# Indexer queries from position 64 on, with both activation parts in one matmul

## The chip, the cores and the metric

The kernel runs on one core of a Trainium2 chip. The metric is the time of one execution on the device in microseconds; the time before is the median of three runs.

## What is computed

One decoder layer over 272 positions (16 meta tokens and 256 of the sequence) of width 2048: sparse attention over a shared latent, a pooling branch, an output projection, a gated feed-forward network and two normalisations. The part that matters here is the indexer, which chooses 64 keys for each query (`top_k = min(256, 256 // 4)`):

```python
dots = jnp.einsum('bqhd,bsd->bqhs', qi, k_idx)
score = jnp.einsum('bqhs,bqh->bqs', jax.nn.relu(dots), wi).astype(jnp.float32)
causal = key_pos[None, :] <= t[:, None]
score = jnp.where(causal[None], score, NEG_INF)
_, sel = lax.top_k(score, top_k)
```

`qi` is the layer's input times 1024 columns of `w_in`, 16 heads of 64. A query at a position below 64 has no more than 64 admissible keys, so all of them are chosen whatever the scores are, and the others are masked again when the logits are made.

## The kernel before, in words

Float32 operands are cut into an upper part, rounded to the chip's `float32r` format (the shapes say fp32r), and a lower part, the rest; a product is the sum of upper by upper, upper by lower and lower by upper. ScalarE makes the upper part of each weight tile (L185) and VectorE the lower one by a subtraction (L186), in two pieces a tile; the tile is called `whl`, its raw form `wraw`. SyncE issues the loads of weight tiles of 1 MB (L191). Three raw and three cut tiles are held at a time, so a tile's cutting can begin when TensorE is done with the tile three before.

The input's cut parts stay in SBUF as 16 K steps (`x_parts`, tile name `xp`, class `Parts`): two stretches of 272 columns, 274 apart. `product` (L288 to L300) runs over K steps and issues three matmuls for each.

The indexer's queries are made in eight tiles of 128 rows, two heads each (the loop over `j` below). A query tile accumulates in PSUM (`mm`) over 16 K steps of three matmuls with 256 columns, for the positions from 16 on. Then ScalarE rounds each head's half to `qi` (L485) and VectorE subtracts it for the lower part (L487); `qi` holds, for a head, the upper part on 64 partitions and the lower on the other 64. While tile j is made, `dots` (L451 to L466) takes the two heads of tile j − 1: head 0 after nine K steps, head 1 after twelve. A head's four matmuls (L460, L461) multiply `qi` with the indexer's keys `kidx`: two for the first 128 queries with 256 key columns, of which 144 are read, and two for the others with 272. ScalarE applies the relu (L463, L464) and VectorE adds to `score` (L466).

During tile 0 and 1 the latent is normalised as well, and in tile 2 TensorE makes a small bias product (L441) from two small loads, `rb_sb` and `oh`, that SyncE issues on the same queue as the weights (L437, L439). The small buffers called "t" (`rl`, `rb_sb`, `oh` and others) are four. After the eight tiles follow the key product (L501 to L503, with the last dot products between), the value product, the choice of keys on VectorE (L554, L555) beside the projection of the attention queries, and all the rest of the layer.

Each engine runs its own instructions in order. That order is made by the tile framework when the program is built, from the order of the code, the edges between tiles, and the free buffers.

Of the kernel before, what the change touches and what calls it, by code (L numbers as in the profile page):

```python
# [11 lines left out]
F32 = mybir.dt.float32  # L12
F32R = mybir.dt.float32r
AF = mybir.ActivationFunctionType
ALU = mybir.AluOpType
AX = mybir.AxisListType

P = 128
D = 2048
NM = 16  # L20
S = 256
T = NM + S
Q0 = NM - 2
NQ = T - Q0
KT = D // P
# [4 lines left out]
DI = 64  # L30
WINS = (2, 4, 8, 16)
TOPK = min(256, S // 4)
FF = 5632
FT = FF // P
PARTS = (8, 8, 8, 8, 8, 4)
# [8 lines left out]
KA = NM + P  # L44
# [23 lines left out]
class Split:  # L68
# [3 lines left out]
    def __init__(self, tile, upper, lower, turned=False, lead=None, early=False, steps=0):  # L72

        self.tile, self.places, self.turned, self.lead, self.early, self.first = tile, (upper, lower), turned, lead, early, P * steps

    def __getitem__(self, key):
        rows, part, c = key
        o = self.places[part]
        if self.lead is not None:
            n = self.first  # L80
            assert c.stop <= n or c.start >= n
            o = self.lead + (n + 64) * part if c.stop <= n else self.places[0] + n + 128 + (2048 - n) * part
        return self.tile[rows, o + c.start:o + (2 * 1024 + 2 if c.stop is None else c.stop)]


class Parts:


    def __init__(self, slot, first, width, apart=274):
        flat = slot.rearrange("p a b -> p (a b)")  # L90
        self.parts = [flat[:, a:a + width] for a in (first, first + apart)]

    def __getitem__(self, key):
        return self.parts[key[1]][key[0], key[2]]
# [35 lines left out]
K_PROJ = (1, 3, 5, 7, 9, 11, 13, 15, 0, 2, 4, 6, 8, 10, 12, 14)  # L130
# [5 lines left out]
def tile_layer(ctx, tc, xt, w_first, w_proj, w_uk, w_uv, w_pool, w_o, w_up, w_down, cols, rows, rel_bias, onehot, out):  # L136
    nc = tc.nc
# [7 lines left out]
    def big():  # L145
        return pm.tile([P, 512], F32, tag="mm", name="mm")

    def small():
        return pa.tile([P, 512], F32, tag="at", name="at")
# [3 lines left out]
    ps = small()  # L153
# [9 lines left out]
    for item in plan:  # L163
# [3 lines left out]
        elif item[0] == "down":  # L167
            n = PARTS[FAST]
# [42 lines left out]
    def split_tile(where=(0, 2048)):  # L211

        return Split(wp.tile([P, 4288], F32R, tag="whl", name="whl"), *where)
# [44 lines left out]
    def weights(ahead=2):  # L258
        i = state["use"]
        state["use"] += 1  # L260
        prefetch(i + 1 + ahead)
        return ready.pop(i)
# [26 lines left out]
    def product(ps, hl, act, lo, hi, places, ks=None, k0=0, k1=KT, firsts=()):  # L289

        for n in range(k0, k1):
            k = (places if ks is None else ks)[n]
            w = slice(P * places.index(k), P * places.index(k) + P)
            wh, wl = hl[:, 0, w], hl[:, 1, w]
            ah, al = act[k][:, 0, lo:hi], act[k][:, 1, lo:hi]
            turned = hl.early if hl.lead is not None and w.start < hl.first else hl.turned
            turn = firsts[n] if n < len(firsts) else "hlx" if turned else "hxl"
            terms = {"h": (wh, ah), "x": (wh, al), "l": (wl, ah)}
            for i, (a, b) in enumerate(terms[t] for t in turn):
                nc.tensor.matmul(ps, a, b, start=n == 0 and i == 0, stop=i == 2 and n == KT - 1)  # L300

    at = ctx.enter_context(ExitStack())
    ap_ = at.enter_context(tc.tile_pool(name="attn", bufs=1))


    x_parts, first = [], []
    for k0, k1 in [(k, k + 1) for k in range(9)] + [(9, 12), (12, 15), (15, 16)]:
# [6 lines left out]
        if k0 % 6 == 0:  # L314
            hl = split_tile()
        for w in ((slice(0, T), slice(T, T + MF)) if k0 == 0 else (slice(0, T + MF),)):
            nc.sync.dma_start(raw[:, k0 % 3:k0 % 3 + k1 - k0, w], w_first[k0:k1, :, w].rearrange("k p c -> p k c"))
        for k in range(k0, k1):
            xk, wk, a0 = raw[:, k % 3, :T], raw[:, k % 3, T:], k % 6 // 3 * 1024 + k % 3 * MF
            c = slice(a0, a0 + MF)  # L320
            a = Parts(ring.tile([P, 2, WIDE], F32R, tag="act", name="xp"), 20, T)
# [35 lines left out]
    def temp(shape, name):  # L357
        return ap_.tile(shape, F32, tag="t", name=name, bufs=4, padded_shape=[P, KW])
# [6 lines left out]
    for k, (hl, a0) in enumerate(first):  # L365
# [4 lines left out]
        for t, (ps, a, m) in terms:  # L370
            nc.tensor.matmul(ps[:m, :T], hl[:, t // 2, a0 + a:a0 + a + m], x_parts[k][:, t % 2, :],  # L371
                             start=k == 0 and t == 0, stop=k == KT - 1 and t == 2)
    ps = heads[0][0]
# [5 lines left out]
    for i in range(2):  # L379
        nc.vector.tensor_tensor(kidx[DI * i:DI * i + DI, 1 + i, :], ps[:DI, :T], kidx[:DI, 0, :].bitcast(F32),  # L380
                                op=ALU.subtract)
# [14 lines left out]
    for j in range(2):  # L396
        ps = heads[1 + j][0]
# [6 lines left out]
    ps = small()  # L404
# [7 lines left out]
    def latent_scale():  # L412
        r = temp([P, W], "r")
        to_partitions(r, sum_rows(sqs))
        nc.vector.tensor_scalar(v, r[:, ::32], 1.0 / C, EPS, op0=ALU.mult, op1=ALU.add)
        nc.gpsimd.tensor_tensor(v, v, half, op=ALU.pow)

    def latent_norm():
        rb = temp([P, W], "rb")
        to_row(rb, v)  # L420
        for j in range(2):
            nc.vector.scalar_tensor_tensor(ct[:, j, :], ct[:, j, :], col(G_KV, j), rb[:, :T], op0=ALU.mult,
                                           op1=ALU.mult)
            nc.scalar.activation(ctp[:, j, 0, :], ct[:, j, :], AF.Copy)
            nc.vector.tensor_tensor(ctp[:, j, 1, :], ct[:, j, :], ctp[:, j, 0, :].bitcast(F32), op=ALU.subtract)
# [28 lines left out]
    def dots(j, qi, pa_, heads, buffer=small):  # L454

        for i in heads:
            h = 2 * j + i
            pb = buffer()
            for o, n, t in ((pa_[:, S * i:S * i + S], S, slice(0, P)), (pb[:, :T], T, slice(P, S))):
                nc.tensor.matmul(o, qi[:, i, t], kidx[:, 0, :n], start=True, stop=False)  # L460
                nc.tensor.matmul(o, qi[:, i, t], kidx[:, 1 + i, :n], start=False, stop=True)  # L461
            rl = temp([P, KW], "rl")
            nc.scalar.activation(rl[:, :KA], pa_[:, S * i:S * i + KA], AF.Relu)  # L463
            nc.scalar.activation(rl[:, KA:], pb[:, :T], AF.Relu)  # L464
            for i2, (a, b) in enumerate(((0, KA), (KA, KW))):
                nc.vector.scalar_tensor_tensor(score[:, a:b], rl[:, a:b], widx[:, i2, h:h + 1], score[:, a:b],  # L466
                                               op0=ALU.mult, op1=ALU.add)

    queries = sb.tile([P, 2, 2, S], F32R, name="qi", tag="y", padded_shape=[P, 2, 2, KT * T // 4])
    qis = []  # L470
    for j in range(8):
        hl = weights()
        ps = big()
        product(ps[:, :S], hl, x_parts, NM, T, K_PROJ, k1=9)
        if j:
            pa_ = small()
            dots(j - 1, qis[j - 1], pa_, (0,))
        product(ps[:, :S], hl, x_parts, NM, T, K_PROJ, k0=9, k1=12)
        if j:
            dots(j - 1, qis[j - 1], pa_, (1,))  # L480
        product(ps[:, :S], hl, x_parts, NM, T, K_PROJ, k0=12)
        qi = queries[:, j % 2]
        for i in range(2):
            r, o = slice(DI * i, DI * i + DI), slice(DI - DI * i, 2 * DI - DI * i)
            query = nc.scalar.activation(qi[r, i, :], ps[r, :S], AF.Copy)  # L485
            query = getattr(query, "ins", query)
            nc.vector.tensor_tensor(qi[o, i, :], ps[r, :S], qi[r, i, :].bitcast(F32), op=ALU.subtract)  # L487
        qis.append(qi)
        if j == 0:
            latent_scale()  # L490
        if j == 1:
            latent_norm()
            relative_bias()
# [3 lines left out]
    for h in range(H):  # L497
        ps = small()
        for c in range(2):
            w = slice(1024 * c + h * HD, 1024 * c + h * HD + HD)  # L500
# [20 lines left out]
    for i, (a, b) in enumerate(((0, NM), (NM, NM + P), (NM + P, T))):  # L521
# [6 lines left out]
        for g in range(2):  # L528
            ps = small()
            for c in range(2):  # L530
                w = slice(1024 * c + 512 * g, 1024 * c + 512 * g + 512)
# [7 lines left out]
            w = slice(512 * g, 512 * g + 512)  # L539
# [10 lines left out]
    src = score  # L550
    for r in range(TOPK // 8):
        for a, b in ((0, KA), (KA, KW)):
# [10 lines left out]
    for h in range(H):  # L563
        hl = weights()
        ps = big()
# [5 lines left out]
    ps = small()  # L571
# [120 lines left out]
    for h in range(H):  # L692
# [3 lines left out]
        hl = weights()  # L696
        ps = big()
# [74 lines left out]
    for m in range(1, KT):  # L772
# [5 lines left out]
        if m == KC:  # L778
            ps = small()
# [151 lines left out]
    gated, todo, both, pair, downs = [], [], [], None, None  # L931
    for item in plan:
# [3 lines left out]
        if item[0] == "down":  # L936
            _, part, c, g = item
            hl = weights()
# [6 lines left out]
            n = PARTS[part]  # L945
            for k in range(4 * g, 4 * g + 4):
                w = slice(512 * (k - 4 * g), 512 * (k - 4 * g) + 512)
                for i in range(2):
                    a, r = pairs[part][k // 2][f"a{i + 1}{k % 2 + 1}"]
# [10 lines left out]
        if half_ == 0:  # L960
            if f % 2 == 0:
                pair = fp.tile([P, 2, S], F32, name="za", tag="z0", bufs=3)
            both = []
        hl = weights()
        ps = big()

        b = 2 * (f - FOLDED) + half_
# [12 lines left out]
        if todo and f > FOLDED + half_:  # L980
            p, r = todo.pop(0)
            with behind(state["use"]):
                pairs[p].append(forms(r, len(pairs[p]), p == FAST))
        if f < FOLDED:
            k = 0
            if f + half_ == 0:
                product(ps[:, :NE], hl, folded, 0, NE, K_UP, k1=5)
                deviation()
                k = 5
# [7 lines left out]
            both = [conv(i * FT + f, i, unfold(both[i]), pair[:, f % 2]) for i in range(2)]  # L997
# [7 lines left out]
        if part > FAST:  # L1005
            a = fp.tile([P, 2, WIDE], F32R, name="gp", tag="gp", bufs=16)
# [5 lines left out]
    n = PARTS[-1]  # L1012
# [3 lines left out]
    for r in range(2):  # L1016
        for c in range(4):
            t = fp.tile([P, 512], F32, name="gb", tag="gp", bufs=16, padded_shape=[P, 2 * WIDE])
# [82 lines left out]
    for i in range(2):  # L1101
        t, mv = slice(i * P, (i + 1) * P), mvs[i]
        waiting = []
        for q, (a, b) in enumerate(cuts[i]):
            ps = small() if i else big()
# [96 lines left out]
```

## Time and profile before

| | |
|---|---|
| median of 3 runs | 1019.71 us (1019.67 to 1019.96) |
| span of the profiled execution | 1019.7 us |
| TensorE matmul busy | 1011.8 us, 99% |
| TensorE weight loads busy | 964.3 us, 95% |
| VectorE busy | 889.8 us, 87% |
| ScalarE busy | 619.5 us, 61% |
| GpSimd busy | 193.4 us, 19% |

The profile lists each engine's busy time, the chain of work that ended last, groups of equal instructions and a timeline with starts from the span's beginning. For the profiled execution it gives the span alone, the time from the first to the last instruction. Matmuls are pipelined: a matmul's recorded length is longer than the distance to the next one's start, so paces are read from starts. In rows, PE is TensorE, PEld its weight loads, DVE VectorE, ACT ScalarE, POOL GpSimd, SP SyncE, and a q behind a name is that engine's queue.

### The profile page before, as it was taken

To read this page: it belongs to the slowest core of one execution; us is meant where nothing else is said; L and a number is where in the kernel's file an instruction comes from. 1 tells how busy PE (TensorE), PEld (TensorE's weight loads), DVE (VectorE), ACT (ScalarE), POOL (GpSimd) and SP (SyncE) were. 2 spreads that over 40 slices of the span, in tenths; PEclk is the share of its full clock that TensorE was granted. 3 is DMA by queue.
4 is the path that set the end of the run, shared out by engine and by line. 5 is a ranking of instruction groups with operands and counts; after the bars stand their busy time and mean duration, and the time that the engine had idled before them with its cause. 6 is when DMAs were issued, how large, how long until landed. Compare 5 with 4: busy or idle time off the path is not lost.

```text
span 1019.7 us, 19201 instructions
## 1 busy us (share of the span) xinstructions
PE 1011.8 (99%) x7644; PEld 964.3 (95%) x7644; DVE 889.8 (87%) x1401; ACT 619.5 (61%) x1000; POOL 193.4 (19%) x245
## 2 busy tenths in 40 slices
PE   9999999999999999999999999999999999999997
PEld 9999999999999999999999999999999999999986
DVE  6878668758869998999999999999999999999876
ACT  7666446645548756655665656656556565666665
POOL 1200014125430021112121111211112111220031
PEclk9999999999999999999999999999999999999999
DMA  9755643354553569899888798887988879888565
GB/s 332 255 190 205 245 148 113 137 187 166 207 206 125 205 197 274 267 370 312 275 281 279 278 304 276 287 276 277 300 281 282 279 279 299 280 285 277 202 218 160
DMA packets 59754, 250.28 MB, mean 245 GB/s; under 512 B 21734, under 2 KB 22416, under 8 KB 32656
## 3 DMA queue, kind: packets, MB, share of 16 engines
q1 hardware_dynamic: 34592, 230.42, 62.2%
q0 software_dynamic: 7888, 16.14, 8.3%
q10 hardware_dynamic: 17184, 2.49, 1.5%
q8 instruction: 60, 0.98, 0.4%
q14 instruction: 30, 0.25, 0.1%
HBM read 232.50 MB, written 2.11 MB: 230 GB/s over the span
## 4 chain that ended last, share of the span: by engine, by line
PE 94%; issue 2%; DVE 1%; DMA 1%; POOL 1%; ACT 0%; POOLq 0%; SPq 0%; DVEq 0%; ACTq 0%
PE mm L300 71%; PE at L899 6%; PE at L898 6%; PE at L900 6%; PE mm L371 2%; DMA wraw<-in_w_down 1%; DVE whl L186 1%; POOL gb L1021 0%; PE mm L599 0%; PE at L460 0%; PE at L634 0%; PE at L461 0%; PE at L346 0%; DVE whl_r L235 0%; DMA wraw<-in_w_first 0%
## 5 line engine op out<-in xcount | busy, mean ns | idle before, releaser
L300 PEld LDWEIGHTS mm<-hp,whl 128*128 128x128 f32 x3840 | 456.9, 188 | 6.3
L300 PE MATMUL mm<-hp,whl 128*128 128x258 f32 x3840 | 458.9, 279 | 0.0
L186 DVE TENSOR_TENSOR whl<-wraw,whl 128x1024 fp32r<-128x1024 f32 (+2 forms) x312 | 370.9, 1216 | 36.9 <-ACT whl L185 35.8
L185 ACT ACTIVATE whl<-wraw 128x1024 fp32r<-128x1024 f32 (+2 forms) x312 | 304.1, 1021 | 76.3 <-PE mm L300 24.6
L300 PE MATMUL mm<-xp,whl 128*128 128x256 f32 (+5 forms) x1152 | 147.1, 284 | 0.0
L300 PEld LDWEIGHTS mm<-xp,whl 128*128 128x128 f32 x1152 | 140.2, 188 | 1.5 <-issue 0.5
L186 DVE TENSOR_TENSOR whl<-room,whl 128x512 fp32r<-128x512 f32 (+1 forms) x104 | 117.8, 1162 | 1.9 <-ACT whl L185 1.6
L185 ACT ACTIVATE whl<-room 128x512 fp32r<-128x512 f32 (+1 forms) x104 | 98.4, 993 | 14.8 <-DVE room L197 7.5
L829 ACT ACTIVATE z<-mm,cv 128x256 f32<-128x256 f32 x40 | 22.6, 565 | 89.7 <-PE mm L300 89.7
L871 POOL TENSOR_TENSOR forms<-za 128x128 f32<-128x128 f32 x20 | 20.4, 1018 | 293.1 <-DVE za L847 228.3
L829 ACT ACTIVATE za<-mm,cv 128x256 f32<-128x256 f32 x40 | 22.6, 565 | 85.1 <-PE mm L300 83.7
L899 PE MATMUL at<-whl,gp 128*128 128x512 f32 x180 | 70.6, 393 | 0.0
L900 PE MATMUL at<-whl,gp 128*128 128x512 f32 x180 | 70.4, 392 | 0.0
L898 PE MATMUL at<-whl,gp 128*128 128x512 f32 x180 | 68.7, 392 | 0.0
L874 POOL TENSOR_TENSOR forms<-za 128x128 f32<-128x128 f32 x20 | 24.4, 1222 | 196.9 <-DVE za L847 144.3
L300 PE MATMUL mm<-mixp,whl 128*128 128x258 f32 x384 | 48.5, 281 | 0.0
L300 PE MATMUL mm<-mixa,whl 128*128 128x258 f32 x384 | 47.8, 280 | 0.0
L300 PEld LDWEIGHTS mm<-mixp,whl 128*128 128x128 f32 x384 | 46.5, 188 | 0.1
L300 PEld LDWEIGHTS mm<-mixa,whl 128*128 128x128 f32 x384 | 46.3, 188 | 0.0
L300 PE MATMUL mm<-fold,whl 128*128 128x260 f32 x384 | 45.8, 280 | 0.0
L300 PEld LDWEIGHTS mm<-fold,whl 128*128 128x128 f32 x384 | 45.5, 187 | 0.1
L900 PEld LDWEIGHTS at<-whl,gp 128*128 128x128 f32 x180 | 33.9, 188 | 7.2
(335 smaller groups left out, 1343.8 us busy)
## 6 DMA issues: line engine op xcount, KB each, us to landing
wraw<-in_w_up SPq DMA_DIRECT2D x62, 1024.0 KB, 5.3
wraw<-in_w_down SPq DMA_DIRECT2D x54, 1024.0 KB, 6.3
room<-in_w_up SPq DMA_DIRECT2D x26, 1024.0 KB, 5.1
room<-in_w_down SPq DMA_DIRECT2D x26, 1024.0 KB, 6.5
wraw<-in_w_proj SPq DMA_DIRECT2D x24, 1024.0 KB, 5.0
wraw<-in_w_o SPq DMA_DIRECT2D x16, 1024.0 KB, 4.8
y<-v POOLq DMA_DIRECT2D x27, 256.0 KB, 8.3
y<-u POOLq DMA_DIRECT2D x18, 256.0 KB, 5.0
```

Source lines behind the costliest of these rows:

```text
L185: upper = nc.scalar.activation(hl[:, 0, c], raw[:, c], AF.Copy)
L186: lower = nc.vector.tensor_tensor(hl[:, 1, c], raw[:, c], hl[:, 0, c].bitcast(F32), op=ALU.subtract)
L300: nc.tensor.matmul(ps, a, b, start=n == 0 and i == 0, stop=i == 2 and n == KT - 1)
L371: nc.tensor.matmul(ps[:m, :T], hl[:, t // 2, a0 + a:a0 + a + m], x_parts[k][:, t % 2, :], start=k == 0 and t == 0, stop=k == KT - 1 and t ...
L829: nc.scalar.activation(z, src[:, 2:NQ], AF.Identity, bias=col(C_B, j), scale=col(C_W, 3 * j + 2))
L871: nc.gpsimd.tensor_tensor(s[:, 0], a21, a22, op=ALU.add)
L874: nc.gpsimd.tensor_tensor(s[:, 3], a11, a21, op=ALU.subtract)
L898: nc.tensor.matmul(ps, a[:, 0, i], hl[:, 0, w], start=j == 0, stop=False)
L899: nc.tensor.matmul(ps, a[:, 0, i], hl[:, 1, w], start=False, stop=False)
L900: nc.tensor.matmul(ps, a[:, 1, i], hl[:, 0, w], start=False, stop=j == n - 1)
```

## The change

Queries are made for the 208 positions from 64 on (`NI = 272 − 64`); the first 48 columns of `qi` are cleared once. For each K step one matmul multiplies the upper weight part with both activation parts side by side, 2 × 208 columns, and a second one adds the lower weight part times the upper activation part, 208 columns, to the second half of the same PSUM range. After the 16 steps ScalarE copies the second half to SBUF (`whole`), VectorE adds the first, and rounding and subtraction read `whole` where they read PSUM. The dot products of the first 128 queries use 144 key columns in place of 256.

```diff
+ALL = TOPK - NM
+NI = S - ALL
...
+        self.whole = (flat, first, apart)
+
+    def both(self, lo, hi):
+
+        flat, first, apart = self.whole
+        return flat[:, first:first + 2 * apart].rearrange("p (a b) -> p a b", b=apart)[:, :, lo:hi]
...
+    def paired(ps, hl, act, lo, hi, places, k0=0, k1=KT):
+
+        m = hi - lo
+        for n in range(k0, k1):
+            k = places[n]
+            w = slice(P * n, P * n + P)
+            nc.tensor.matmul(ps[:, :2 * m], hl[:, 0, w], act[k].both(lo, hi), start=n == 0, stop=False)
+            nc.tensor.matmul(ps[:, m:2 * m], hl[:, 1, w], act[k][:, 0, lo:hi], start=False, stop=n == KT - 1)
+
...
-            for o, n, t in ((pa_[:, S * i:S * i + S], S, slice(0, P)), (pb[:, :T], T, slice(P, S))):
+            for o, n, t in ((pa_[:, S * i:S * i + KA], KA, slice(0, P)), (pb[:, :T], T, slice(P, S))):
...
+    nc.gpsimd.memset(queries[:, :, :, :ALL].bitcast(F32), 0.0)
...
-        product(ps[:, :S], hl, x_parts, NM, T, K_PROJ, k1=9)
+        paired(ps, hl, x_parts, TOPK, T, K_PROJ, k1=9)
...
-        product(ps[:, :S], hl, x_parts, NM, T, K_PROJ, k0=9, k1=12)
+        paired(ps, hl, x_parts, TOPK, T, K_PROJ, k0=9, k1=12)
...
-        product(ps[:, :S], hl, x_parts, NM, T, K_PROJ, k0=12)
+        paired(ps, hl, x_parts, TOPK, T, K_PROJ, k0=12)
         qi = queries[:, j % 2]
+        whole = temp([P, NI], "whole")
+        nc.scalar.activation(whole, ps[:, NI:2 * NI], AF.Copy)
+        nc.vector.tensor_tensor(whole, ps[:, :NI], whole, op=ALU.add)
         for i in range(2):
             r, o = slice(DI * i, DI * i + DI), slice(DI - DI * i, 2 * DI - DI * i)
-            query = nc.scalar.activation(qi[r, i, :], ps[r, :S], AF.Copy)
+            query = nc.scalar.activation(qi[r, i, ALL:], whole[r], AF.Copy)
             query = getattr(query, "ins", query)
-            nc.vector.tensor_tensor(qi[o, i, :], ps[r, :S], qi[r, i, :].bitcast(F32), op=ALU.subtract)
+            nc.vector.tensor_tensor(qi[o, i, ALL:], whole[r], qi[r, i, ALL:].bitcast(F32), op=ALU.subtract)
```

The change also moves instructions, because the framework orders them anew. (Line numbers after the change are higher: L186 is now L194, L191 is L199, L466 is L483, L487 is L508.) On VectorE, at the end of a middle tile, there stood before the change:

```order
L466 SCALAR_TENSOR_TENSOR score<-rl,widx,score 128x272
L487 TENSOR_TENSOR qi<-mm,qi 64x256
L186 TENSOR_TENSOR whl<-wraw,whl 128x1024
L487 TENSOR_TENSOR qi<-mm,qi 64x256
L186 TENSOR_TENSOR whl<-wraw,whl 128x1024
L466 SCALAR_TENSOR_TENSOR score<-rl,widx,score 128x144
```

and now there stands:

```order
L483 SCALAR_TENSOR_TENSOR score<-rl,widx,score 128x272
L503 TENSOR_TENSOR whole<-mm,whole 128x208
L194 TENSOR_TENSOR whl<-wraw,whl 128x1024
L508 TENSOR_TENSOR qi<-whole,qi 64x208 x2
L194 TENSOR_TENSOR whl<-wraw,whl 128x1024
L483 SCALAR_TENSOR_TENSOR score<-rl,widx,score 128x144
```

The subtraction for head 0 was ahead of the first half of the weight split and is now behind it; the add of the two ranges has its old place. On ScalarE it is alike: copy, first half of the split, then both roundings. After tile 6, on VectorE, the split has pieces of 512 and 1536 columns, and the rows now are:

```order
L503 TENSOR_TENSOR whole<-mm,whole 128x208
L194 TENSOR_TENSOR whl<-wraw,whl 128x512
L194 TENSOR_TENSOR whl<-wraw,whl 128x1536
L508 TENSOR_TENSOR qi<-whole,qi 64x208 x2
L483 SCALAR_TENSOR_TENSOR score<-rl,widx,score 128x144
```

Both pieces are now ahead of the subtractions; before, head 0's stood ahead of both and head 1's behind both. On SyncE, where the stage's loads are issued, there stood before:

```order
L331 DMA cv<-in_cols 128x394
L191 DMA wraw<-in_w_proj 128x2048 x6
L437 DMA rb_sb<-in_rel_bias 32x8
L439 DMA oh<-in_onehot 32x272
L191 DMA wraw<-in_w_proj 128x2048 x2
```

and now:

```order
L348 DMA cv<-in_cols 128x394
L199 DMA wraw<-in_w_proj 128x2048 x7
L454 DMA rb_sb<-in_rel_bias 32x8
L456 DMA oh<-in_onehot 32x272
L199 DMA wraw<-in_w_proj 128x2048
```

The two small loads are now issued after the seventh weight tile in place of the sixth.

## Rows read from the trace of the kernel before

**Rows 1.** The page, part 4: the chain that ended last, shares by engine.
```profile
PE 94%; issue 2%; DVE 1%; DMA 1%; POOL 1%; ACT 0%; POOLq 0%; SPq 0%; DVEq 0%; ACTq 0%
```

**Rows 2.** Busy time by stretch: length, engines (instructions), granted clock, DMA share, GB/s.
```profile
23.00:30.00 7.00, 7.00 (x56) 6.63 (x56) 6.91 (x10) 6.22 (x12) 0.00 (x0) 1.00 0.77 253
...
70.20:77.20 7.00, 6.88 (x59) 6.71 (x58) 4.88 (x8) 3.83 (x8) 0.00 (x0) 1.00 0.52 186
```

**Rows 3.** Timeline, TensorE, tiles 2 and 3: start us, length us, engine, line.
```profile
42.51 4.71 PE L300 MATMUL mm<-xp,whl 128*128 128x256 f32 x39
...
47.06 0.28 PE L460 MATMUL at<-kidx,qi 128*128 128x256 f32 x1
...
47.54 1.21 PE L300 MATMUL mm<-xp,whl 128*128 128x256 f32 x9
...
49.08 2.05 PE L300 MATMUL mm<-xp,whl 128*128 128x256 f32 x16
```

**Rows 4.** Timeline, TensorE, feed-forward part: four matmuls of 512 columns, then another.
```profile
404.60 0.39 PE L899 MATMUL at<-whl,gp 128*128 128x512 f32 x1
...
405.51 0.28 PE L300 MATMUL mm<-hp,whl 128*128 128x258 f32 x1
```

**Rows 5.** Weight loads by shape: count | busy us, mean ns of one | idle before.
```profile
L300 PEld LDWEIGHTS mm<-xp,whl 128*128 128x128 f32 x1152 | 140.2, 188 | 1.5 <-issue 0.5
...
L573 PEld LDWEIGHTS at<-kt,qt 128*2 128x2 f32 x16 | 0.5, 82 | 0.3
```

**Rows 6.** Timeline, ScalarE and VectorE at the end of tile 2.
```profile
44.13 0.38 ACT L485 ACTIVATE qi<-mm 64x256 fp32r<-64x256 f32 x1 [1.03 <-PE mm L300]
...
44.42 1.05 ACT L185 ACTIVATE whl<-wraw 128x1024 fp32r<-128x1024 f32 x1
44.55 0.42 DVE L487 TENSOR_TENSOR qi<-mm,qi 64x256 fp32r<-64x256 f32 x1 [0.31 <-ACT qi L485]
...
45.50 1.23 DVE L186 TENSOR_TENSOR whl<-wraw,whl 128x1024 fp32r<-128x1024 f32 x1 [0.53 <-ACT whl L185]
```

**Rows 7.** Timeline, VectorE in tiles 0 and 1, and TensorE's first dot products.
```profile
26.80 3.49 DVE L186 TENSOR_TENSOR whl<-wraw,whl 128x1024 fp32r<-128x1024 f32 x3
...
30.76 0.48 DVE L351 STREAM_TRANSPOSE r<-at 128x288 f32<-128x288 f32 x1
...
33.13 0.28 PE L460 MATMUL at<-kidx,qi 128*128 128x256 f32 x1
```

**Rows 8.** DMA issues from 18 to 48 us (us to landing); timeline of tile 2, TensorE.
```profile
wraw<-in_w_proj SPq DMA_DIRECT2D x6, 1024.0 KB, 5.1
...
oh<-in_onehot SPq DMA_DIRECT2D x1, 34.0 KB, 1.9
...
38.06 0.62 PE L441 MATMUL at<-oh,rb_sb 32*8 32x272 f32 x2
...
40.49 0.28 PE L460 MATMUL at<-kidx,qi 128*128 128x256 f32 x1
```

**Rows 9.** Timeline of tile 7: ScalarE, VectorE, TensorE.
```profile
70.77 2.00 ACT L185 ACTIVATE whl<-wraw 128x512 fp32r<-128x512 f32 x2
...
72.80 1.76 DVE L186 TENSOR_TENSOR whl<-wraw,whl 128x1536 fp32r<-128x1536 f32 x1 [0.69 <-ACT whl L185]
...
74.59 0.43 DVE L487 TENSOR_TENSOR qi<-mm,qi 64x256 fp32r<-64x256 f32 x1
...
75.16 0.35 PE L460 MATMUL at<-kidx,qi 128*128 128x256 f32 x1
...
77.18 0.28 PE L501 MATMUL at<-ctp,whl 128*128 128x272 f32 x1
```

**Rows 10.** Timeline, TensorE: a plain float32 product, two records of one matmul.
```profile
147.27 0.41 PE L598 MATMUL mm<-kt,qt 128*128 128x144 f32 x2
147.51 0.62 PE L599 MATMUL mm<-kt,qt 128*128 128x272 f32 x2
```

**Rows 11.** Timeline, TensorE between the key product's heads.
```profile
80.86 0.39 PE L460 MATMUL mm<-kidx,qi 128*128 128x256 f32 x1
```

## The prediction

> **What bounds the kernel now.** I read the page first: 94% of the chain that ended last is TensorE's work [rows 1]. That says where time can be saved, not that a saving arrives. So the second view is the table of stretches: in the stage of the eight query tiles TensorE has hardly any idle time at the full granted clock, 2.4 GHz, but VectorE is nearly full too in the first stretch (6.91 of 7 us) and 70% full in the last one, 4.88 of 7 [rows 2]. The third view is the timeline of one tile, for the two numbers on which all rests: how fast TensorE streams, and how long before it needs a result that result is there.
>
> Streaming: 39 matmuls of 256 columns start within 47.06 − 42.51 us, 116.7 ns each [rows 3]; 512 columns take (405.51 − 404.60)/4 = 227.5 ns [rows 4]. A line through both gives 0.433 ns a column: 186 ns for 416 columns, and 96 for 208 if the line goes on below 256, which no row shows.
>
> Let E be the moment when a tile's last product has streamed and the next tile may begin. For tile 2, E = 42.51 + 12 × 0.1167 = 43.91 us; for tile 3, 49.08 + 12 × 0.1167 = 50.48: a period of 6.57 us [rows 3]. TensorE comes to head 0's dot products at 47.06 = E + 3.15. What they need is done at 44.55 + 0.42 = E + 1.06 [rows 6]: 2.1 us of slack, because the first subtraction stands ahead of the weight split on VectorE.
>
> **The change, part by part.**
>
> *K steps.* Three matmuls of 256 columns (350 ns) become one of 416 and one of 208. The narrow one lasts 96 ns by the line, but each matmul has a weight load of its own, and those loads last 188 ns for 128 columns and 82 for 2 [rows 5]: 0.84 ns a column above a fixed part, 108 ns for 128 columns. A load that has only a 208-column matmul to hide behind would set the pace. I take 108, because a 256-column matmul's 117 hides exactly such a load now; the bounds are 96 and 117. A K step is then 294 ns, 56 less than before. Over 8 × 16 steps TensorE has 7.2 us less to do (8.7 at 96 ns, 6.0 at 117). The Trainium skill ("TensorE: Matmul & The Clock Gate", LDWEIGHTS) has a load last its columns divided by 1.2 GHz, 107 ns for 128, and so speaks against this change where the line of rows alone does not; by the rule the sum below is 1020.3, by the line 1019.0.
>
> *Dot products.* 32 matmuls of 256 columns become 144: about 10 ns less each at the load's pace, 0.3 us; on the line 32 × (117 − 68) = 1.6.
>
> *The end of a tile.* Now ScalarE copies the second range (0.35 us, a little under the 0.38 of 256 columns), VectorE adds (0.37, as the old subtraction's 0.42 of 256 columns), ScalarE rounds, VectorE subtracts (0.37 each) [rows 6]. And VectorE's queue has the half weight split *between* the add and both subtractions, as the order shows. From E: ScalarE's copy ends at 0.22 + 0.35 = 0.57; the add runs from 0.60 to 0.97; ScalarE's half split starts 0.25 after the copy's start, lasts 1.05 and ends at 1.53; VectorE's half runs from 1.56 to 2.79; the subtraction to 3.19; TensorE starts 0.14 after that (75.16 against 74.59 + 0.43) [rows 9]: E + 3.33. Its nine K steps take 9 × 0.294 = 2.65. So it waits 0.7 us in each tile, and the period is 3.33 + 2 × 0.46 for the heads' dot products (0.48 now [rows 3]) + 7 × 0.294 = 6.31: **0.26 less than before, not 0.9**. VectorE's queue is the bound.
>
> *Tiles 0 and 1.* Tile 0 saves 16 × 56 ns = 0.9 us. But VectorE splits weights until 30.29 in any case [rows 7]; then add 0.37, transposition 0.48, half split 1.23, subtraction 0.37 and gaps end at 32.85, and the dot products start at 33.0 against 33.13: only 0.1 is left. Seven K steps to the tile's end bring 0.4. Balance −0.5.
>
> *Tile 2.* Here TensorE has the small bias product (L441), which needs two small transfers. On SyncE's queue they now stand behind the seventh weight tile instead of the sixth, as the order shows. That tile is issued when VectorE has finished the next half split: 32.85, second subtraction 0.40 with its gap, about 0.17 of small work, 1.23, so 34.7; 5.1 us to landing gives 39.8, and the small ones land behind it [rows 8]. TensorE would be there at about 37.6 (33.0 + 2 × 0.46 + 7 K steps, then five and a wide matmul) and sits until 39.9, where it passed at 38.06 before; then 0.55 for the product, a narrow matmul and three K steps to the dot products: 41.5 against 40.49, **+1.0**. (If they did not queue behind the tile, the second would land 1.9 us after an issue near 35.5, and the term would be −0.4; VectorE's subtractions near 39 hide under this wait and would then be next.) Seven K steps and the dot products bring 0.5 back: balance +0.5.
>
> *Tiles 3 to 6.* 4 × −0.26: balance −0.5.
>
> *Tile 7.* The split queued here has a piece of 512 and one of 1536, and now both stand ahead of the subtractions: ScalarE's two last 2.00 us and end at E + 2.47, VectorE's large one 1.76 more, the subtraction ends at 4.65, the dot products start at E + 4.8. Before, head 0 passed freely and only head 1 waited, and the tile lasted from 70.20 (50.48 and three periods) to 77.18, 6.98 us [rows 9]; now 4.8 + 0.92 + 2.06 = 7.78, **+0.8**: balance +0.3.
>
> *After the tiles.* ScalarE rounds the last tile only after VectorE's add, so its copies of the keys begin about 0.3 later. TensorE already waits in this place (the matmul at 80.86 is 0.39 long where its like are 0.28) [rows 11] and would wait that much more: balance +0.6. Behind it TensorE has the order of before, so the shift stays to the end. POOL's new clearing of 48 columns hides in its idle time (0.00 busy until 30 us [rows 2]); without that cover it would delay tile 0's first rounding, where VectorE is busy until 30.29 anyway.
>
> Sum: the balance runs −0.5, +0.5, −0.5, +0.3 and ends at **+0.6 us**. Against the profiled execution's 1019.7 (the median of the runs is 1019.71) that is **1020.3 us**. At 96 ns a narrow matmul the period is 3.33 + 2 × 0.39 + 7 × 0.282 = 6.08 and the same walk ends at −0.7 (1019.0); at 117, at +1.3 (1021.0). A measurement of this kernel can tell 0.2%, 2.0 us, from no change. With half a microsecond either way for the waits that I worked out, the forecast's own range is 1018.0 to 1021.7.
>
> **The rivals.**
>
> *The work saved arrives.* If the first subtraction ended before E + 2.6 in every tile and the small transfers came in time, TensorE's 7.2 + 0.3 us would come off but for the 0.3 at the end: 1012.5; at 96 ns, 1009.7. For it: TensorE is the engine without idle time [rows 2]. Against: VectorE's 1.23 us in its queue's order, which needs ScalarE's 1.05 first.
>
> *Narrow matmuls run at another pace (the slower side).* A plain float32 matmul of 144 columns is two records that take 0.24 us together [rows 10], 1.69 ns a column. Were the rounded format to fall to that pace below 256 columns, a narrow matmul would last 352 ns: 128 × (352 + 186 − 350) = +24 us and 32 × (244 − 117) ns = +4 for the dot products, with no wait for VectorE left: about 1048. For it: every rounded matmul of the weights that I found has 256 columns or more. Against: 256 and 512 lie on a line that nearly meets zero, as one pass does. It decides from about 128 ns a narrow matmul on, since each 10 ns above mine cost 0.7 us.
>
> *The waits cost the clock.* TensorE would have two waits of some 2 us where it now has none. If the granted clock fell to 1.2 GHz after one for half a tile, 24 of the old matmuls' work would take 117 ns longer each: +2.8, 1023. Against: the clock is 1.00 in every stretch, the last one with short waits included [rows 2]. That idle gaps between bursts lower it is what the same page of the Trainium skill says ("Why this matters for your kernels"); no row here has such a gap.
>
> *The wide matmul gains nothing.* If its two pieces, 274 columns apart, stream like two matmuls, a K step is 2 × 117 + 108 = 342 ns, and mostly the waits stay: 1022.4.
>
> **How the numbers follow.** Forecast 0.70; work arrives 0.13; slow narrow matmuls 0.06; clock 0.06; wide gains nothing 0.05. The first lies within 0.2%, the second is faster, the others slower: 0.13, 0.70, 0.17. The range takes the forecast's own, half a microsecond more below for waits partly escaped, and above reaches to the wide matmul's and the clock's cases: 1017.5 to 1023.0. Left out are the full saving and the slow pace, 0.19.
>
> **What would show it.** TensorE idle for 0.7 us before the first dot products of each tile, released by VectorE's subtraction; a wait of over 2 us at the bias product, for a transfer; the longest wait for VectorE in tile 7; matmuls of 208 columns spaced 108 ns, weight loads still 188. Wrong if tiles come 5.6 us apart, or if narrow matmuls are spaced over 130 ns.

## The result and the profile after

| | before | after |
|---|---|---|
| median of the runs | 1019.79 us (4) | 1025.88 us (4; 1024.10 to 1026.09) |
| ratio, 95% interval | | 1.0055 [1.0041, 1.0069] |
| span of the profiled execution | 1019.7 us | 1024.3 us (its own time 1026.09) |

The change is slower by 0.55%, outside the range of the prediction. Where the time goes is seen by the start of the same work on TensorE, read from both timelines (a line of dot products is that of head 0):

| TensorE starts | before, us | after, us | shift |
|---|---|---|---|
| query tile 0 | 22.95 | 23.50 | +0.55 |
| dot products in tile 1 | 33.13 | 32.79 | −0.34 |
| in tile 2 | 40.49 | 44.84 | +4.35 |
| in tile 3 | 47.06 | 52.84 | +5.78 |
| in tile 6 | 66.78 | 72.11 | +5.33 |
| in tile 7 | 73.35 | 80.03 | +6.68 |
| key product | 77.18 | 83.18 | +6.00 |
| value product | 84.47 | 91.16 | +6.69 |
| attention queries | 91.87 | 98.57 | +6.70 |
| end of the span | 1019.7 | 1024.3 | +4.6 |

Nearly all is lost in one tile and a half: 6.1 of the 6.7 us lie between the dot products in tile 1 and those in tile 3. The chain that ended last, after (answers to [rows 1]): 4% of it have gone from TensorE to other engines and to transfers. That is where the path now runs, not time lost.

```profile
PE 90%; DVE 3%; DMA 3%; issue 2%; ACT 1%; POOL 1%; SPq 0%; POOLq 0%; ACTq 0%; DVEq 0%
```

Busy time by stretch, after, columns as in [rows 2] (the number before the DMA share is the granted clock):

```profile
23.00:30.00 7.00, 6.72 (x45) 6.22 (x43) 6.83 (x9) 6.49 (x12) 0.00 (x0) 1.00 0.71 224
36.50:44.00 7.50, 3.41 (x15) 2.24 (x14) 5.69 (x11) 3.17 (x6) 2.15 (x3) 0.85 0.42 137
44.00:50.50 6.50, 6.50 (x32) 6.41 (x32) 2.03 (x5) 2.04 (x6) 2.88 (x4) 0.65 0.55 185
...
46.00:47.50 1.50, 1.50 (x7) 1.45 (x7) 0.64 (x2) 0.39 (x1) 0.14 (x1) 0.50 0.13 47
...
50.50:57.00 6.50, 6.16 (x43) 5.86 (x42) 5.12 (x10) 4.38 (x10) 0.00 (x0) 1.00 0.95 274
```

From 36.5 to 44 us TensorE is busy for 3.41 of 7.5 us. In the next stretch it is busy throughout, but at a mean granted clock of 0.65, and does 32 matmuls where a stretch of that length at 1.00 has 43 and waits besides; within it, from 46 to 47.5, the clock is 0.50, the lower level of 1.2 GHz. The timeline of TensorE there:

```profile
37.37 0.36 PE L316 MATMUL mm<-xp,whl 128*128 128x416 f32 x1
41.83 1.06 PE L458 MATMUL at<-oh,rb_sb 32*8 32x272 f32 x2 [4.09 <-DMA oh<-in_onehot]
42.81 0.54 PE L317 MATMUL mm<-xp,whl 128*128 128x208 f32 x1
43.16 0.59 PE L316 MATMUL mm<-xp,whl 128*128 128x416 f32 x1
43.54 0.38 PE L317 MATMUL mm<-xp,whl 128*128 128x208 f32 x1
43.72 0.59 PE L316 MATMUL mm<-xp,whl 128*128 128x416 f32 x1
...
48.63 0.26 PE L317 MATMUL mm<-xp,whl 128*128 128x208 f32 x1
48.73 0.37 PE L316 MATMUL mm<-xp,whl 128*128 128x416 f32 x1
48.94 0.26 PE L317 MATMUL mm<-xp,whl 128*128 128x208 f32 x1
49.04 0.36 PE L316 MATMUL mm<-xp,whl 128*128 128x416 f32 x1
```

The small bias product waits 4.09 us for `oh`. Behind it a K step takes 43.72 − 43.16 = 0.56 us, from 48.7 on 49.04 − 48.73 = 0.31: TensorE runs at 1.2 GHz for some 6.5 us after the wait, then at 2.4 again. SyncE's queue from 33 to 36 us shows what was late, first the start of the weight tile's issue, then the issues with the time to landing in us:

```profile
34.21 0.33 SPq L199 DMA_DIRECT2D wraw<-in_w_proj  x1
...
wraw<-in_w_proj SPq DMA_DIRECT2D x1, 1024.0 KB, 7.1
...
oh<-in_onehot SPq DMA_DIRECT2D x1, 34.0 KB, 5.9
rb_sb<-in_rel_bias SPq DMA_DIRECT2D x1, 1.0 KB, 6.6
```

The seventh weight tile, issued at 34.21, took 7.1 us, and the small ones, issued at 34.91 and 35.80, landed at 41.5 and 41.7, right behind it. Before, `oh` took 1.9 us [rows 8]. There too it landed right behind its tile, the sixth, but that was issued at 30.31 us and had landed at 36.4. The stretches show which part of the transfer was long (the last two columns are the DMA share and GB/s):

```profile
36.25:38.75 2.50, 1.49 (x10) 1.20 (x8) 2.46 (x5) 2.45 (x7) 0.00 (x0) 1.00 0.86 343
38.75:41.25 2.50, 0.00 (x0) 0.00 (x0) 2.38 (x7) 0.97 (x2) 1.12 (x2) 1.00 0.07 25
```

By 38.75 us most of the tile had come. In the 2.5 us after that the rate was 25 GB/s at a DMA share of 0.07, which is about one of the 16 DMA engines (an estimate: 0.07 × 16 = 1.1).

The rest of the stage is as the prediction drew it. VectorE and TensorE at the end of tile 3 and in tile 7, after (answers to [rows 6, 9]):

```profile
56.64 0.38 DVE L503 TENSOR_TENSOR whole<-mm,whole 128x208 f32<-128x208 f32 x1 [0.70 <-ACT whole L502]
57.59 1.23 DVE L194 TENSOR_TENSOR whl<-wraw,whl 128x1024 fp32r<-128x1024 f32 x1 [0.57 <-ACT whl L193]
58.84 0.77 DVE L508 TENSOR_TENSOR qi<-whole,qi 64x208 fp32r<-64x208 f32 x2
59.27 0.34 PE L477 MATMUL at<-kidx,qi 128*128 128x144 f32 x1 [0.36 <-DVE qi L508]
...
77.82 1.76 DVE L194 TENSOR_TENSOR whl<-wraw,whl 128x1536 fp32r<-128x1536 f32 x1 [0.69 <-ACT whl L193]
79.61 0.77 DVE L508 TENSOR_TENSOR qi<-whole,qi 64x208 fp32r<-64x208 f32 x2
80.03 0.34 PE L477 MATMUL at<-kidx,qi 128*128 128x144 f32 x1 [1.84 <-DVE qi L508]
```

The split stands between the add and the subtractions, TensorE waits for the first subtraction in each tile from tile 3 on, and longest in tile 7. And after the tiles, among the key products (answers to [rows 11]):

```profile
87.31 0.33 PE L477 MATMUL mm<-kidx,qi 128*128 128x144 f32 x1 [0.71 <-ACT rl L480]
```

### The profile page after: what moved, and what is told of

Same layout as the page of the kernel before. It is cut to its first block, busy times and chain, and to the rows that moved or that the text cites. A ratio compares the mean times of both kernels' runs of the same rounds, so it can differ in the third digit from the quotient of the medians.

```text
span 1024.3 us, 18956 instructions
## 1 busy us (share of the span) xinstructions
PE 1008.5 (98%) x7516; PEld 958.8 (94%) x7516; DVE 892.2 (87%) x1409; ACT 622.4 (61%) x1008; POOL 190.7 (19%) x246
## 4 chain that ended last, share of the span: by engine, by line
PE 90%; DVE 3%; DMA 3%; issue 2%; ACT 1%; POOL 1%; SPq 0%; POOLq 0%; ACTq 0%; DVEq 0%
PE mm L308 66%; PE at L920 6%; PE at L919 6%; PE at L921 6%; DVE whl L194 1%; PE mm L316 1%; ACT whl L193 1%; DMA wraw<-in_w_proj 1%; PE mm L317 1%; DMA wraw<-in_w_down 1%; DMA oh<-in_onehot 1%; DMA wraw<-in_w_first 1%; PE at L477 0%; PE mm L620 0%; PE at L478 0%
## 5 line engine op out<-in xcount | busy, mean ns | idle before, releaser
L194 DVE TENSOR_TENSOR whl<-wraw,whl 128x1024 fp32r<-128x1024 f32 (+2 forms) x312 | 370.6, 1215 | 34.3 <-ACT whl L193 33.3
L194 DVE TENSOR_TENSOR whl<-room,whl 128x512 fp32r<-128x512 f32 (+1 forms) x104 | 118.0, 1164 | 1.9 <-ACT whl L193 1.6
L308 PE MATMUL mm<-xp,whl 128*128 128x258 f32 (+4 forms) x768 | 98.8, 285 | 0.0
L308 PEld LDWEIGHTS mm<-xp,whl 128*128 128x128 f32 x768 | 93.8, 188 | 0.9
L316 PE MATMUL mm<-xp,whl 128*128 128x416 f32 x128 | 41.7, 381 | 0.0
```

The source lines that it names most:

```text
L194: lower = nc.vector.tensor_tensor(hl[:, 1, c], raw[:, c], hl[:, 0, c].bitcast(F32), op=ALU.subtract)
L316: nc.tensor.matmul(ps[:, :2 * m], hl[:, 0, w], act[k].both(lo, hi), start=n == 0, stop=False)
```

## The experiments

The theory after this reading: the wait for the small transfer and the clock's fall behind it are the loss; the order on VectorE costs half a microsecond a tile besides. Each run is compared with the kernel before measured beside it, whose median was 1021.14 us for the first four runs and 1020.27 for the last four.

**loads_early.** The loads are issued before the first weight tile:

```diff
+    rb_sb = ap_.tile([32, H], F32, name="rb_sb")
+    nc.sync.dma_start(rb_sb, rel_bias)
+    oh = ap_.tile([32, T], F32, name="oh")
+    nc.sync.dma_start(oh, onehot)
+
     def relative_bias():
-        rb_sb = temp([32, H], "rb_sb")
-        nc.sync.dma_start(rb_sb, rel_bias)
-        oh = temp([32, T], "oh")
-        nc.sync.dma_start(oh, onehot)
         ps = small()
```

> The changed kernel; only the two small loads are issued before the first weight tile, into buffers of their own. Theory: the 6.1 us lost are the wait of TensorE for the small transfer in tile 2 (4.1 us from 37.74 to 41.83) and the stretch after it in which TensorE is granted 1.2 GHz (41.8 to 48.3, half of 6.5 us, so 3.2 us lost); both go, so no wait over 1 us in tile 2, clock 1.00 from 23 us on, and 1025.9 - 4.1 - 3.2 = 1018.6 us, with 0.5 us either way for VectorE's work of tile 2 that hid under the wait. Rival 1 (VectorE is the bound of the whole stage, the wait only shows where its lateness is taken up): the time is lost again in the later tiles, 1023 us or more. Rival 2 (the clock falls from the new pattern of wide and narrow matmuls with short waits, not from the long wait): 1.2 GHz shows somewhere between 30 and 80 us all the same, 1021.8 us.

Measured: 1024.33 us, 1.0034 [1.0021, 1.0047] of before: some 2 us better than the changed kernel stands against before, not 7; that is the time of rival 1. The walk says where they went. The profiled execution is itself a late one (1025.78 us; tile 0 starts at 25.16, 1.66 us later than in the changed kernel); with that taken off, the dot products in tile 1 are 1.53 us later than in the changed kernel, those in tile 3 5.60 us earlier. Between the two lie tile 2's wait and the slow clock: 7.13 us gained, as the theory had it.

```profile
35.98 0.33 PE L478 MATMUL at<-kidx,qi 128*128 128x144 f32 x1 [0.91 <-DVE qi L509]
48.90 0.33 PE L478 MATMUL at<-kidx,qi 128*128 128x144 f32 x1 [0.30 <-DVE qi L509]
```

Some of it was lost again in three other places. In tile 1 ScalarE's queue was in the wrong order at the wrong time:

```profile
31.39 0.34 ACT L503 ACTIVATE whole<-mm 128x208 f32<-128x208 f32 x1
33.20 1.06 ACT L193 ACTIVATE whl<-wraw 128x1024 fp32r<-128x1024 f32 x1 [1.47 <-DMA wraw<-in_w_proj]
34.17 0.76 ACT L507 ACTIVATE qi<-whole 64x208 fp32r<-64x208 f32 x2
```

The weight split waited 1.47 us for its transfer, and the rounding stood behind it. The transfer was late because the order changed further ahead as well: the second half of the first weight tile's split now stands behind the indexer's keys (`kidx`) on both engines and ended at 28.32 us (24.08 in the changed kernel), and the fourth tile was issued at 28.34 (24.11), with the 1.66 taken off still 2.6 us later. In tile 3 the second dot products waited for a relu (0.7 us lost to the next tile). And in tile 7, after the same 1.8 us wait for VectorE that the changed kernel has, the clock fell here (1.5 us lost by the key product):

```profile
77.00:84.00 7.00, 7.00 (x42) 6.90 (x43) 3.00 (x8) 3.03 (x9) 0.00 (x0) 0.76 0.45 152
```

So the 7 us are real, and the order on ScalarE and VectorE, with the clock's fall behind it, took more than half of them back (1.53 + 0.7 + 1.5).

**split_after_rounding.** Only the order is changed, by an edge from the last tile's rounding to the next split (`query` is ScalarE's second rounding):

```diff
+    rounded = []
...
-            parts = split_part(raw, hl, slice(a, b))
+            parts = split_part(raw, hl, slice(a, b), rounded[-1:])
+        rounded.clear()
...
         qis.append(qi)
+        rounded.append(query)
```

> The changed kernel; only the order is changed: the weight split of the next tile but two stands behind the rounding of the query tile on ScalarE, and so behind the subtractions on VectorE. The small loads are late as in the changed kernel. Theory: the waits before the dot products (0.34 to 0.36 us idle in tiles 3 to 6, in starts 0.5 us, and 1.84 in tile 7) go; four periods fall from 6.42 to 5.9 us (2.1 us), tile 7 from 7.9 to about 6 (1.9), the wait in tile 2 and the 1.2 GHz stretch stay: 1025.9 - 4.0 = 1021.9 us. Rival 1 (VectorE's total work sets the pace of the tiles, whatever its order): periods stay at 6.4, 1025.9 us. Rival 3 (what is put off comes back: the split ends later, so the raw buffer comes free later, the weight tiles arrive later and TensorE waits for a cut tile instead): new waits for the weights' tile, 1024 us or more.

Measured: 1020.98 us, 0.9997 [0.9988, 1.0007]: no slower than the kernel before. In tiles 4 to 6 the dot products stand 5.95 us apart (54.10, 60.05, 66.02), no wait for VectorE's subtractions is left, and no row shows TensorE waiting for a cut weight tile: rivals 1 and 3 fall.

```profile
60.05 0.24 PE L480 MATMUL at<-kidx,qi 128*128 128x144 f32 x1
66.02 0.24 PE L480 MATMUL at<-kidx,qi 128*128 128x144 f32 x1
```

The gain against the changed kernel is some 5.5 us where 4.0 was expected; in the profiled execution, the fastest of all (1018.05 us), the wait was still there, but the clock did not fall:

```profile
40.82 0.61 PE L461 MATMUL at<-oh,rb_sb 32*8 32x272 f32 x2 [2.79 <-DMA oh<-in_onehot]
```

```profile
36.50:44.00 7.50, 4.71 (x32) 3.98 (x31) 6.84 (x15) 4.27 (x9) 1.40 (x3) 1.00 0.33 132
44.00:50.50 6.50, 6.50 (x48) 6.43 (x47) 4.16 (x8) 4.70 (x11) 2.47 (x3) 1.00 0.96 348
```

In most of its other executions it seems to have fallen: the mean granted clock over the whole run was 0.998 in this one and 0.994 in four others, and these took 1020.99 to 1021.21 us. That is 3.1 us between executions of one program that differ in the clock. Where it fell in them is not on record, and executions of the kernel before that agree in the clock to 0.001 lie up to 2.5 us apart, so the 3.1 us can't be put down to the clock alone.

**early_and_after_rounding.** Both edits.

> The changed kernel with both edits: small loads first, weight split behind the rounding. Theory: the gains add up, no wait over 1 us in the query tiles, clock 1.00, periods of 5.9 us against 6.57 before the change: 1025.9 - 7.3 - 4.0 = 1014.6 us, 0.5% under the kernel before. Rival 1 (VectorE bound): about 1018.6 or more. Rival 3 (late weight tiles): 1017 or more with waits for cut weight tiles.

Measured: 1017.99 us, 0.9974 [0.9963, 0.9985]: 2.7 us faster than before. The theory had 5.1 (1019.7 − 1014.6). Periods are 5.96 us (58.68 to 64.64), the clock is 1.00 in every stretch to 92 us, and no wait over 0.75 us is left. The attention queries start at 89.40, 9.2 us earlier than in the changed kernel, where the theory had 7.3 + 4.0 = 11.3. Of the 2.1 us between them 0.7 are missing up to the dot products in tile 3 (46.27), and 1.1 from there to the key product (73.68), half of it in the first of these periods, 6.45 us with a wait for a relu. The last 0.3 lie behind the tiles: from the first key product to the attention queries it took 15.72 us, 15.39 in the changed kernel and 14.69 before. There ScalarE's copies of the keys now stood behind the rounding *and* a split of two pieces:

```profile
74.72 0.78 ACT L510 ACTIVATE qi<-whole 64x208 fp32r<-64x208 f32 x2 [0.44 <-DVE whole L507]
75.53 2.01 ACT L193 ACTIVATE whl<-wraw 128x512 fp32r<-128x512 f32 x2
77.44 0.66 ACT L531 ACTIVATE kt<-at 128x272 f32<-128x272 f32 x2
```

**wait_filled.** TensorE gets 48 matmuls of constants to do while it waits for the small load:

```diff
         ps = small()
+        for _ in range(48):
+            nc.tensor.matmul(ps[:, :256], warm[:, :P], warm, start=True, stop=True)
         nc.tensor.matmul(ps[:H, :T], rb_sb, oh, start=True, stop=True)
```

> The changed kernel; only 48 matmuls of constants (256 columns, bf16, about 107 ns each at 2.4 GHz) are put into the small product's PSUM range right ahead of it, which overwrites them, so that TensorE streams while it waits for the small transfer. Theory: the wait's end stays near 41.8 us but the granted clock stays at 2.4 GHz, so 3.2 us come back: 1025.9 - 3.2 = 1022.7 us. Rival 2 (the clock falls from the pattern of matmuls, or from what comes later, not from the idle time): it is at 1.2 GHz for some 6 us all the same and the time stays at 1025.9 us or is above it.

Measured: 1025.65 us, 1.0048 [1.0033, 1.0063]: the total is rival 2's, the clock is the theory's.

```profile
36.33 5.55 PE L459 MATMUL at<-const-bfloat16-1.0 128*128 128x256 bf16 x48
42.44 0.61 PE L460 MATMUL at<-oh,rb_sb 32*8 32x272 f32 x2 [0.55 <-DMA oh<-in_onehot]
```

```profile
36.50:44.00 7.50, 6.95 (x57) 5.64 (x56) 6.13 (x12) 3.62 (x7) 1.98 (x3) 1.00 0.49 152
44.00:50.50 6.50, 6.50 (x47) 6.41 (x46) 2.20 (x6) 2.78 (x7) 3.03 (x4) 1.00 0.51 185
```

With TensorE busy up to the product, the clock stays at 1.00 in this execution; over the whole of each of the four executions its mean was 0.995 to 0.998, against 0.994 to 0.996 in the changed kernel's four. The total hides it, because the framework put the product 5.5 K steps earlier: work that the changed kernel does ahead of the wait comes behind it here (5.5 × 0.303 = 1.7 us), and the product ran 0.6 us later, with `oh`. The clock's price by itself is read from the product to the dot products in tile 3:

```profile
52.20 0.30 PE L479 MATMUL at<-kidx,qi 128*128 128x144 f32 x1 [0.39 <-DVE qi L510]
```

It takes 52.20 − 42.44 − 1.7 = 8.1 us here and 52.84 − 41.83 = 11.0 in the changed kernel: **2.9 us**.

**early_and_after_rounding_2.** The kernel with both edits, and in it:

```diff
-        rounded.append(query)
+        if j < 7:
+            rounded.append(query)
```

> As the kernel with early loads and the split behind the rounding, but the split that is queued at the end of tile 7 (pieces of 512 and 1536 columns) stands behind the rounding of tile 6 and not of tile 7. There it held up ScalarE's copies of the keys: from the first key product to the first matmul of the attention queries 15.72 us went by (73.68 to 89.40) against 14.69 before the change. Theory: that 1.0 us comes back, the query tiles keep periods of 5.95 us, so 3.7 us less than the kernel before in the same call. Rival: beside tile 7's dot products the two pieces hold up the last rounding instead, and the stage ends where it did: 2.7 us less than the kernel before.

Measured: 1017.02 us, 0.9966 [0.9952, 0.9979], 3.2 us under the kernel before by the medians (3.1 for the run with both edits) and the best median of all. Between 2.7 and 3.7 the times don't decide; the rows speak for the rival, since the stage took as long (73.74 to 89.57, 15.83 us), now with a wait of 1.0 us for a relu:

```profile
78.31 0.33 PE L481 MATMUL mm<-kidx,qi 128*128 128x144 f32 x1 [0.95 <-ACT rl L484]
```

How it would come free was not tried.

**range_alone.** The best order, but three narrow matmuls for each K step and no sum:

```diff
-        paired(ps, hl, x_parts, TOPK, T, K_PROJ, k1=9)
+        product(ps[:, :NI], hl, x_parts, TOPK, T, K_PROJ, k1=9)
...
-        whole = temp([P, NI], "whole")
-        nc.scalar.activation(whole, ps[:, NI:2 * NI], AF.Copy)
-        nc.vector.tensor_tensor(whole, ps[:, :NI], whole, op=ALU.add)
+        whole = ps[:, :NI]
```

> Queries from 64 on as three matmuls of 208 columns for each K step in place of one of 416 and one of 208, read from PSUM as in the kernel before, with the early loads and the split behind the rounding of the kernel run with it. This measures narrow matmuls back to back. Theory (a narrow one streams at the line's pace, 96 ns, whatever is loaded): K step 3 x 97 = 291 ns where the pair takes 303, 128 x 12 ns = 1.5 us faster than the paired kernel, and no copy and add on the way. Rival (weight loads set the pace of narrow matmuls behind one another, 108 ns): K step 324 ns, 2.7 us slower than the paired kernel.

Measured: 1019.41 us, 0.9989 [0.9979, 0.9999], 2.4 us slower than the paired kernel measured beside it: the rival was right. Nine matmuls of 208 columns start within 56.65 − 55.66 = 0.99 us, 110 ns each, where the line through 256 and 512 columns has 96:

```profile
55.66 1.15 PE L311 MATMUL mm<-xp,whl 128*128 128x208 f32 x9
56.65 0.25 PE L481 MATMUL at<-kidx,qi 128*128 128x144 f32 x1
```

So of the 3.2 us that the best order brings, about one is the shorter range, and some two are the pairing with its copy and sum.

**after_again and before_again.** The same two kernels once more.

> The changed kernel once more. Theory: the wait for the small transfer in tile 2 (about 4 us) and the fall to 1.2 GHz behind it belong to this program: 1.0055 of the kernel before, 5.6 us. Rival: both were an accident of one chip or one execution; without the clock's fall it would be 3 us less, 1.0025.

Measured: 1025.82 us, 1.0049 [1.0036, 1.0062]. The wait was 3.3 us, and the clock fell again:

```profile
36.50:44.00 7.50, 4.19 (x20) 3.00 (x19) 6.37 (x13) 3.62 (x7) 2.33 (x4) 0.78 0.44 146
44.00:50.50 6.50, 6.50 (x35) 6.39 (x35) 2.12 (x5) 2.45 (x6) 2.56 (x4) 0.72 0.42 156
```

> The kernel before once more, for its profile. From 91.87 us (the first matmul of the attention queries) to the end it took 927.8 us, the changed kernel 925.7 for the same work, because a period in which matmuls of 258 columns are spaced 122 ns instead of 115.6 ended at about 238 us there and at 217 here (210 by the place in the program). Theory: that period comes and goes by itself; in this execution of the same kernel it ends elsewhere, and the rest lasts 925.5 to 928. Rival: it belongs to the program: 927.8 us and an end at 238 us again.

Measured in one execution: span 1018.6 us; from the first attention query (92.61 us) to the end 926.0 us, not 927.8. In the first execution the period of 122 ns still lasted at 220 us: 24 matmuls of one tile started within 220.88 − 217.95 = 2.93 us; in this one the same 24 within 221.34 − 218.57 = 2.77 us.

```profile
217.95 3.10 PE L300 MATMUL mm<-mixp,whl 128*128 128x258 f32 x24
220.88 3.10 PE L300 MATMUL mm<-mixa,whl 128*128 128x258 f32 x24
```

```profile
218.57 2.94 PE L300 MATMUL mm<-mixp,whl 128*128 128x258 f32 x24
221.34 2.94 PE L300 MATMUL mm<-mixa,whl 128*128 128x258 f32 x24
```

So the 2 us by which the shift seemed to shrink after 98.57 us need not belong to the change: two executions of one kernel differ by as much.

## Why the prediction was wrong, step by step

- **Tile 2: the step that failed, in two terms.** That the small transfers would stand behind the seventh tile and hold TensorE was right, and so was the time when TensorE would be there (37.6; 37.74 in the trace). The first term is the transfer: the tile was reckoned at 5.1 us to landing and took 7.1. It was issued 0.5 us earlier than reckoned and the small ones landed up to 0.4 us behind it, so the product ran at 41.83 and not at 39.9: 1.9 us more. Why that transfer was longer is open. With the same order of loads the tile took 6.4 us in `after_again`, 7.3 in `wait_filled` and 5.2 in `split_after_rounding`, so one figure of 5.1 was too narrow a basis.
- **The clock: the second term, which the sum had at nothing.** The fall was a consequence of the wait, not a rival to it. The forecast itself held a wait of 2.3 us in tile 2, and the clock's fall stood beside it as another case with a chance of 0.06. "The clock is 1.00 in every stretch" was no evidence: no row of before has such a wait. The price agrees, 2.8 us against 2.9, partly by luck: that it would last half a tile was taken from no row. Whether it would have fallen after the 2.3 us of the forecast no run shows; after 2.79 us it did not in the one execution that was profiled. The Trainium skill ("TensorE: Matmul & The Clock Gate", "Why this matters for your kernels") says that idle gaps between bursts lower the clock. After a wait of 4.09 us this trace agrees, and filling the wait shows that the idle time is the cause.
- **K steps.** 303 ns where 294 were taken, inside the bounds but at the upper one (117 ns a narrow matmul, +0.7 us in the sum). In the pair a narrow one lasts 96 ns to the next start, and the wide one 206 instead of the line's 186. Back to back narrow ones take 110, nearer to the weight load's 108 than to the line's 96. The Trainium skill's rule ("TensorE: Matmul & The Clock Gate", LDWEIGHTS) gives 107 for the load; the 110 ns of `range_alone` lie near it, though a load's row is 188 ns long.
- **The end of a tile.** Right: dot products at E + 3.26 in tile 4 (E = 56.01, 3.33 forecast) and at E + 4.74 in tile 7 (E = 75.29, 4.8 forecast). The idle rows say 0.36 us because a matmul's recorded length reaches beyond its streaming; by starts it is 0.53. The period is 6.42, 6.31 forecast: a gain of 0.15 a tile, not 0.26.
- **Tiles 0 and 1, tile 7.** The dot products in tile 1 came 0.34 us earlier, 0.1 forecast. Tile 7 lasted 83.18 − 75.29 = 7.89 us, 7.78 forecast: 0.9 us longer than before, 0.8 forecast.
- **After the tiles.** +0.7, +0.3 forecast: right in kind, half in size.

The sum redone: 0.6 + 1.9 (transfer) + 2.9 (clock) + 0.7 (K steps) + 0.4 (after the tiles) = 6.5 us, against a shift of 6.70 at the attention queries and 6.1 between the medians.

The rival that the work saved arrives came nearer than the forecast thought, but only by edits that the change doesn't have: with the loads early and the subtractions ahead of the split, 3.2 of its 7.2 us come.

## What to carry to other kernels

When a change shifts the order of a shared load queue, ask for each small transfer behind a large one who waits for it; a 34 KB load cost 7 us here, more than half of it before and the rest after it had landed. A wait of several microseconds on TensorE, 4.09 us here, is to be priced together with the slower clock behind it, as one case. And a result that the next stage needs should stand ahead of work that has time (a weight split for two tiles on) in every in-order queue it passes; an edge that says so brought more than 5 us.

## What was not expected of the hardware

- The clock's fall is not certain. After a 2.79 us wait it stayed at 1.00 in the profiled execution of `split_after_rounding`. After 1.84 us in tile 7 it fell in `loads_early` (0.76 over 77 to 84 us) and stayed at 1.00 in the changed kernel, `after_again` and `wait_filled`, with the same idle time on the row.
- A narrow matmul between wide ones is not slowed itself (96 ns): the wide one behind it is (206, where the line has 186). That the wide one's weight load, 188 ns on its row, has only the narrow one to hide behind is argued, not shown.
- In all ten profiled executions there is a period, beginning after 140 us and ending between 210 and 245, in which matmuls of 258 columns are spaced 120 to 122 ns instead of 115.6 at a granted clock of 1.00. Its end moves from execution to execution, and with it up to two microseconds of the total (927.8 against 926.0 us for the same work of the kernel before). What makes it is open.
